# A two-layer diffusion trunk on one core: the normalisation moves from GpSimd to VectorE and ScalarE, and modulations change place

## The chip, the cores and the metric

The kernel runs on one core of one Trainium2 chip. The metric is the device time of one execution in microseconds (us). The core has five engines that run beside each other and wait for each other through semaphores: TensorE (PE in the rows, matmuls; its weight loads are PEld), VectorE (DVE), ScalarE (ACT), GpSimd (POOL) and SyncE (SP, which here only issues DMA).

## The reference

One inference step of a trunk with two layers over 128 context tokens and 128 latent tokens, `D_MODEL` 2048, all in fp32. What matters here:

```python
def _modulation(cond, w_mod, b_mod):
    m = jax.nn.silu(cond) @ w_mod + b_mod
    return [t[:, None, :] for t in jnp.split(m, N_MOD, axis=-1)]

def _layer(x, mods, lw, ctx):
    shift1, scale1, gate1, shift2, scale2, gate2 = mods
    ...
    h = _rms_norm(x, lw['norm1_g']) * (1.0 + scale1) + shift1
    gq, gk, gv, gr, glr, aq, ak, av, dqkv, dz, da, db = _split_cols(h @ lw['w_in'])
    ...
    mix = jnp.concatenate([o_gla, o_att, o_dn], axis=-1) @ lw['w_out']
    x = x + gate1 * mix
    h = _rms_norm(x, lw['norm2_g']) * (1.0 + scale2) + shift2
    ff = jnp.square(jax.nn.relu(h @ lw['w_ff1'])) @ lw['w_ff2']
    x = x + gate2 * ff
    return x, (k, v, s_gla.astype(x.dtype), s_dn.astype(x.dtype))
```

Each layer has six modulation vectors of 2048 numbers for each of two conditionings (context and latent). Each is a product of a conditioning vector with a 2048 x 2048 slice of `w_mod`.

## The kernel before

Both token sets are worked on together: a tile of activations holds 128 features by 256 tokens, and 16 such tiles ("chunks" k = 0 to 15) make up the 2048 features. A product in fp32 is made of three products in a faster format. A weight tile of 128 x 1024 is loaded (`raw`), ScalarE rounds it to `hi`, VectorE takes the residue `lo = raw - hi`; the same split of the activations gives a high part (columns 0 to 255 of `act`) and a residue (256 to 511). TensorE then does `hi` with both parts and `lo` with the high part. So each weight tile costs one instruction on ScalarE (`hi<-raw`), one on VectorE (`lo<-raw,hi`) and 24 matmuls.

In order of time: a first phase (0 to about 200 us), the mixing of layer 0 (linear attention, attention and DeltaNet chains woven with projections, to about 500), its output projection (to 592), the **first lead**, the feed-forward of layer 0 (four quarters, first product `ff1(q)`, second `ff2(q)`, to 1392), the **middle lead**, the mixing and output projection of layer 1 (to 1842), the **last lead**, and the feed-forward of layer 1.

A lead (`norm_lead`) is the start of the product behind an RMS norm. So that TensorE need not wait for the norm, the first six units (five in the middle lead) are multiplied with x times its scale alone, 12 weight tiles in all (`gl` in the rows), and brought in order afterwards. Beside this, VectorE turns the mean square (`nv`) into 1/sqrt by Newton's iteration in small steps (`n2t`, `n2y`, then `diag`, which spreads it), and `normed` makes the 16 normalised chunks that all later units need: `ht` is x times rstd, `hu` the chunk with scale and shift, and then its high part (ScalarE, `act<-hu`) and residue (VectorE, `act<-hu,act`). In `normed` GpSimd makes `ht` and half of `hu`. In the two leads ahead of a feed-forward, `sink` sends the six results through relu and square (`ffr`) at the end.

A modulation is computed in one of two ways. `mod_pe` uses TensorE with the conditioning as 32 weight columns: for each of 16 slices of `w_mod` it loads two halves (`raws`) and issues four matmuls at four column positions, a "quad", 512 columns each. The profile records two passes for each such matmul, so a quad is eight records. `mod_dv` uses VectorE: 64 multiply-and-sum instructions (`junk`, the sum goes to `part` or `modc`, each followed by a short read-out), on weights loaded as `mraw` (32 loads of 512 KB). `ONDV` names the four modulations done so: (layer, number) = (0, 5), (1, 1), (1, 0), (1, 5).

When a modulation runs is set by two queues, `modq` (TensorE) and `modv` (VectorE). `start_mod` puts one in; each weight tile of a product calls `tick()`, which adds `rate[0]` and `rate[1]` to two counters and lets a modulation do its next step when its counter reaches one. `FF0M` lists which modulations of layer 1 start in the feed-forward of layer 0, `V3`, `V4` and `V5` are values of `rate[1]`, and `DL` is the number of units of `ff1(0)` ahead of `start_mod`.

This gives the order of the program. The order on each engine is then set by the framework's scheduler when the kernel is built (`TileContext(nc, schedule_with_timeline_sim=True)`): it lets an instruction that is ready go ahead of one that is not, so that pieces of modulations come to stand between other work. A token given to matmuls (`tok`) keeps those with the same token in the order in which they were written.

Of the kernel before, what the change touches and what calls it, by code (L numbers as in the profile page):

```python
# [14 lines left out]
AF = mybir.ActivationFunctionType  # L15
ALU = mybir.AluOpType
AX = mybir.AxisListType
P = 128
# [6 lines left out]
TB = 4  # L25
NRAW = 6
GATES = (4, 5, 6, 7, 0, 1, 2, 3)
V3, V4, V5 = 0.6, 0.7, 0.4
FF0M = (1, 0, 2, 4, 3)
MX1M = (4, 3)  # L30
LATE = 3
ONDV = ((0, 5), (1, 1), (1, 0), (1, 5))
DL = (0, 2)
WIDE = (1,)
K0, K1 = 0.4, 0.7
LEAD, LEAD1, PUMP, SKIP = 6, 5, 2, 2
R1, R2, R3 = 0.9, 0.45, 0.15
# [4 lines left out]
def tile_hybrid_step(ctx: ExitStack, tc: tile.TileContext, A: dict, O: dict):  # L42
    nc = tc.nc
# [16 lines left out]
    ve, se = Timed(nc.vector, 1 / 960, 0.13), Timed(nc.scalar, 1 / 1400, 0.27)  # L60
# [20 lines left out]
    def newtok():  # L81
        ntok[0] += 1
        return f"tok{ntok[0]}"

    def mm(out, lhsT, rhs, start=True, stop=True, tok=None, **kw):
        i = nc.tensor.matmul(out, lhsT=lhsT, rhs=rhs, start=start, stop=stop, **kw)  # L86
        n = math.prod(rhs.shape[1:])
        pe_t[0] += max(n / 2400 * (1 if rhs.dtype == F32R else 4), 0.027)
        if tok is not None:
            tc.stamp_issue_order_token(i.ins, tok)  # L90
        return i
# [21 lines left out]
    def bc(ap, n):  # L113
        s = list(ap.shape)
        return ap.unsqueeze(len(s)).to_broadcast(s + [n])
# [5 lines left out]
    X = {}  # L121
# [88 lines left out]
    def load_half(src, pl=None):  # L210
        raw = (pl or wraw).tile([P, 1024], F32, tag="raw", name="raw")
        nc.sync.dma_start(raw, src)
        return raw
# [25 lines left out]
    rate = [1.0, 0]  # L239
# [94 lines left out]
    def gemm_seq(units, rhs_of, wide=False):  # L334
        for u in units:
            gemm_d([u], rhs_of, 16, wide)
# [90 lines left out]

    def mod_pe(l, m, modc, bm):
        ps = pmod.tile([P, 512], F32, tag="mod", name="mod")
        for k in range(16):  # L430
            raws = [load_half(A["w_mod"][l, m, k, half]) for half in range(2)]
            for gg in range(4):
                mm(
                    ps[32 * gg : 32 * gg + 32, :],
                    sc[:, 2 * k : 2 * k + 32],
                    raws[gg // 2][:, (gg % 2) * 512 : (gg % 2) * 512 + 512],
                    start=(k == 0),
                    stop=(k == 15),
                    tile_position=(0, 32 * gg),
                )  # L440
            yield
        msb = nrm.tile([P, 512], F32, tag="msb", name="msb")
        se.activation(msb, ps, AF.Copy)
        pt = ps
        for r in range(4):
            mm(pt[:, r * 8 : r * 8 + 8], msb[:, r * P : r * P + P], sel8)
        ve.tensor_tensor(
            modc[:, m].rearrange("p (g r) c -> p r g c", r=4),
            pt[:, 0:32].rearrange("p (r g c) -> p r g c", r=4, c=2),
            bc(bm[:, m].rearrange("p (g r) -> p r g", r=4), 2),  # L450
            ALU.add,
        )
        yield
# [38 lines left out]
    def normed(rstd, dst, scl, shf):  # L492
        for k in range(16):
            t = X["np"].tile([P, 256], F32, tag="ht", name="ht", bufs=2)
            u = X["np"].tile([P, 256], F32, tag="hu", name="hu", bufs=2)
            nc.gpsimd.tensor_tensor(t, X["x"][:, k, :], rstd, ALU.mult)  # L496
            if k % 2 == 0:
                nc.gpsimd.tensor_scalar(u[:, 0:P], t[:, 0:P], scl[:, k, 0:1], shf[:, k, 0:1], ALU.mult, ALU.add)
            else:
                se.activation(u[:, 0:P], t[:, 0:P], AF.Identity, scale=scl[:, k, 0:1], bias=shf[:, k, 0:1])  # L500
            ve.tensor_scalar(u[:, P:256], t[:, P:256], scl[:, k, 1:2], shf[:, k, 1:2], ALU.mult, ALU.add)
            se.activation(dst[:, k, 0:256], u, AF.Copy)
            ve.tensor_tensor(dst[:, k, 256:512], u, dst[:, k, 0:256].bitcast(F32), ALU.subtract)
            yield

    def norm_lead(srcs, xsp, dst, scl, shf, ldp, sink=None):
        se.activation(xsp[:, :, 256:258], shf, AF.Copy)
        ve.tensor_tensor(xsp[:, :, 514:516], shf, xsp[:, :, 256:258].bitcast(F32), ALU.subtract)
        rstd = get_rstd()
        return lead_gemm(srcs, xsp, rstd, normed(rstd, dst, scl, shf), ldp, sink)  # L510
# [5 lines left out]
    def start_mod(l, m):  # L516
        modc, s12, bm, ng = mods[l]

        def chain():
            yield from (mod_dv if (l, m) in ONDV else mod_pe)(l, m, modc, bm)  # L520
            if m in (1, 4):
                j = 0 if m == 1 else 1
                ve.scalar_tensor_tensor(
                    s12[:, j].rearrange("p k c -> p c k"), modc[:, m].rearrange("p k c -> p c k"), 1.0,
                    ng[:, j].unsqueeze(1).to_broadcast([P, 2, 16]), ALU.add, ALU.mult,
                )

        g = chain()
        gens[l, m] = g
        (modv if (l, m) in ONDV else modq).append(g)  # L530
        return g

    def tsrc(w, n):
        return lambda half: w[n, half]
# [108 lines left out]
    for l in range(L):  # L643
# [171 lines left out]
        else:  # L815
            nlead = list(zip(FIRST, first))
            for j in FIRST[len(first) : 13]:
                for _ in range(2):
                    if nlead:
                        u, ps = nlead.pop(0)  # L820
# [563 lines left out]
        x = X["x"]  # L1384
# [33 lines left out]
        last = l + 1 == L  # L1418
        hids = [act, hidb]

        def ff_evac(hid, j):
            def f(ps):
                r = X["np"].tile([P, 256], F32, tag="ht", name="ffr", bufs=2)
                r2 = X["np"].tile([P, 256], F32, tag="hu", name="ffr2", bufs=2)
                se.activation(r, ps, AF.Relu)
                se.activation(hid[:, j, 0:256], r, AF.Square)
                se.activation(r2, r, AF.Square)
                ve.tensor_tensor(hid[:, j, 256:512], r2, hid[:, j, 0:256].bitcast(F32), ALU.subtract)

            return f  # L1430

        norm_lead([tsrc(w1, j) for j in range(LEAD)], hidb, nact, s12[:, 1], modc[:, 3], X["np"],
                  lambda j, t: ff_evac(act, j)(t))
        rate[:] = [R3, V4 if last else V3]
        if not last:
            mod_tiles(l + 1)
            layer_consts(l + 1)
# [1 line left out]
        def ff1(q):  # L1439
            hid = hids[q % 2]  # L1440
            us = [(tsrc(w1, q * 16 + j), ff_evac(hid, j)) for j in range(LEAD if q == 0 else 0, 16)]
            if q == 0:
                d = DL[l]
                gemm_seq(us[:d], lambda k: nact[:, k, 0:512])
                us = us[d:]
                if (l, 5) not in gens:
                    start_mod(l, 5)
                if not last:
                    for m in FF0M:
                        start_mod(l + 1, m)  # L1450
            gemm_seq(us, lambda k: nact[:, k, 0:512])
            return hid

        def ff2(q, hid):
            st = q == 3 and not last
            sc1 = mods[l + 1][1][:, 0] if st else None
            gemm_seq([(tsrc(w2[q], n), res_evac(n, 5, act if st else None, sc1)) for n in range(16)], lambda k: hid[:, k, 0:512], l in WIDE)

        h0 = ff1(0)
        h1 = ff1(1)  # L1460
        mod_flush(gens[l, 5])
        rate[1] = 0 if last else V5
        ff2(0, h0)
        h2 = ff1(2)
        ff2(1, h1)
        h3 = ff1(3)
# [186 lines left out]
```

## Time and profile before

| what | value |
|---|---|
| time, median of 3 runs | 2616.69 us (2614.7 to 2617.31) |
| the profiled execution's own time | 2615.59 us |
| its span, first to last instruction | 2613.8 us |
| TensorE busy | 2518.4 us, 96% |
| VectorE busy | 1831.2 us, 70% |
| ScalarE busy | 1208.2 us, 46% |
| GpSimd busy | 121.4 us, 5% |
| mean granted TensorE clock | 0.986 |
| read from HBM | 612.57 MB, 237 GB/s over the span |

Matmuls are pipelined, and the ends of their records are modelled, so a stretch in which TensorE is busy throughout can still hold fewer matmuls than another. The number of records in a stretch, at the pace of a stretch where nothing waits, says how much work was done in it. The granted clock is a share of TensorE's full speed. An idle time is put down to the instruction that ended it.

### The profile page before, as it was taken

What the parts mean: (1) busy time and instruction counts of PE and PEld (TensorE: products, weight loads), DVE (VectorE), ACT (ScalarE), POOL (GpSimd) and SP (SyncE); (2) the same over time, 40 slices, a digit from 0 to 9 for tenths busy, and PEclk for the clock granted to TensorE, in tenths of its full rate; (3) what the DMA queues carried; (4) which work ended last, traced back from release to release, by engine and by line L of the source; (5) the groups of instructions that cost most, each with busy time, mean ns of one, the idle gap of its engine ahead of it and who ended that gap; (6) DMA issues with size and microseconds to landing.
All of it is one profiled execution on the core that took longest, in us unless ns stands there. A gap on an engine that the chain in (4) does not pass through costs nothing.

```text
span 2613.8 us, 47705 instructions
## 1 busy us (share of the span) xinstructions
PE 2518.4 (96%) x18860; PEld 2252.6 (86%) x18860; DVE 1831.2 (70%) x3462; ACT 1208.2 (46%) x1905; POOL 121.4 (5%) x131
## 2 busy tenths in 40 slices
PE   6999999998899999999999999999879999999999
PEld 4777677787899999999998888889869989999988
DVE  3457757799999889444567676889894565564665
ACT  3356244444554354354355653555355535445433
POOL 1000000004000000000004000000120000000000
PEclk9999999999999999999999999999979999999999
DMA  9876767897899998777776764448666666666564
GB/s 352 320 255 211 272 216 255 325 353 243 275 342 334 329 339 299 231 231 226 224 232 221 276 201 125 143 127 295 230 200 187 184 191 188 185 192 187 186 196 142
DMA packets 171937, 622.01 MB, mean 238 GB/s; under 512 B 20497, under 2 KB 21073, under 8 KB 170689
## 3 DMA queue, kind: packets, MB, share of 16 engines
q1 hardware_dynamic: 165600, 600.12, 68.3%
q0 software_dynamic: 3712, 15.59, 1.7%
q8 instruction: 148, 2.42, 0.4%
q10 hardware_dynamic: 2400, 3.24, 0.4%
q14 instruction: 77, 0.62, 0.1%
HBM read 612.57 MB, written 6.31 MB: 237 GB/s over the span
## 4 chain that ended last, share of the span: by engine, by line
PE 85%; issue 6%; DMA 5%; DVE 3%; ACT 1%; SPq 0%; ACTq 0%; DVEq 0%; POOLq 0%
PE g L86 64%; PE gt L86 6%; PE mod L86 5%; DMA raw<-w_tok 1%; DMA sb<-scd 1%; DMA raw<-w_in 1%; DMA raw<-w_mod 1%; DVE junk L56 1%; DVE lo L56 1%; PE ga L86 1%; PE gl L86 1%; PE eb L86 1%; DVE act L56 1%; ACT hi L56 0%; PE fbm L86 0%
## 5 line engine op out<-in xcount | busy, mean ns | idle before, releaser
L56 ACT ACTIVATE hi<-raw 128x1024 fp32r<-128x1024 f32 (+1 forms) x742 | 784.5, 1058 | 1097.5 <-PE g L86 799.9
L56 DVE TENSOR_TENSOR lo<-raw,hi 128x1024 fp32r<-128x1024 f32 (+1 forms) x742 | 908.8, 1225 | 444.9 <-ACT hi L56 433.5
L86 PE MATMUL g<-act,hi 128*128 128x256 f32 (+1 forms) x7488 | 1064.1, 292 | 39.6 <-DVE act L56 17.1
L86 PEld LDWEIGHTS g<-act,hi 128*128 128x128 f32 x7488 | 961.5, 190 | 119.6 <-DVE act L56 22.7
L86 PE MATMUL g<-act,lo 128*128 128x256 f32 x4000 | 563.7, 282 | 0.0
L86 PEld LDWEIGHTS g<-act,lo 128*128 128x128 f32 x4000 | 517.2, 190 | 14.8 <-issue 3.2
L56 DVE SCALAR_TENSOR_TENSOR x<-g,modc,x 128x128 f32<-128x128 f32 x448 | 142.4, 348 | 183.2 <-PE g L86 177.9
L86 PE MATMUL g<-hid,hi 128*128 128x256 f32 (+1 forms) x1536 | 261.2, 319 | 0.0
L86 PEld LDWEIGHTS g<-hid,hi 128*128 128x128 f32 x1536 | 217.0, 188 | 23.9 <-ACT hi L56 5.0
L86 PE MATMUL mod<-raw,sc 128*32 128x512 f32 (+1 forms) x1280 | 164.0, 529 | 24.8 <-DMA raw<-w_mod 20.3
L56 DVE CUSTOM_DVE_ANT_0 junk<-mraw,sb,part 128x1024 bf16<-128x1024 f32 x128 | 170.7, 1334 | 9.6 <-DMA sb<-scd 9.4
L56 DVE CUSTOM_DVE_ANT_0 junk<-mraw,sb,bm 128x1024 bf16<-128x1024 f32 x128 | 163.9, 1281 | 4.0 <-DMA sb<-scd 3.1
L86 PE MATMUL gt<-hi,act 128*128 128x512 f32 x512 | 141.4, 408 | 3.4 <-ACT hi L56 3.4
L86 PE MATMUL g<-hid,lo 128*128 128x256 f32 x1024 | 141.8, 281 | 0.0
L86 PEld LDWEIGHTS g<-hid,lo 128*128 128x128 f32 x1024 | 134.6, 188 | 5.4
L86 PEld LDWEIGHTS gt<-hi,act 128*128 128x128 f32 x512 | 94.0, 190 | 39.6 <-issue 11.7
L86 PEld LDWEIGHTS mod<-raw,sc 128*32 128x32 f32 x1280 | 31.9, 109 | 66.8 <-issue 16.8
L496 POOL TENSOR_TENSOR ht<-x,rstd 128x256 f32<-128x256 f32 x48 | 56.2, 1187 | 480.9 <-ACT rstd L56 461.8
L86 PE MATMUL gl<-hid,hi 128*128 128x258 f32 x384 | 73.9, 294 | 3.4 <-ACT hi L56 2.4
L86 PE MATMUL gt<-lo,act 128*128 128x512 f32 x256 | 75.6, 403 | 0.0
L86 PE MATMUL gl<-hid,lo 128*128 128x258 f32 x192 | 56.7, 295 | 9.4 <-DVE lo L56 9.4
L86 PEld LDWEIGHTS gl<-hid,hi 128*128 128x128 f32 x384 | 62.1, 198 | 4.1 <-ACT hi L56 2.8
(355 smaller groups left out, 1926.6 us busy)
## 6 DMA issues: line engine op xcount, KB each, us to landing
raw<-w_ff SPq DMA_DIRECT2D x512, 512.0 KB, 4.4
raw<-w_mod SPq DMA_DIRECT2D x256, 512.0 KB, 5.8
mraw<-w_modT SPq DMA_DIRECT2D x128, 512.0 KB, 5.1
raw<-w_in SPq DMA_DIRECT2D x86, 512.0 KB, 4.4
raw<-w_tok SPq DMA_DIRECT2D x64, 512.0 KB, 4.8
raw<-w_out SPq DMA_DIRECT2D x64, 512.0 KB, 4.9
sb<-scd POOLq DMA_DIRECT2D x8, 1024.0 KB, 8.9
raw<-w_in SPq DMA_DIRECT2D x16, 448.0 KB, 6.2
```

The lines of the kernel that those rows point to most:

```text
L56: return f(out, *a, **kw)
L86: i = nc.tensor.matmul(out, lhsT=lhsT, rhs=rhs, start=start, stop=stop, **kw)
L496: nc.gpsimd.tensor_tensor(t, X["x"][:, k, :], rstd, ALU.mult)
```

## The change

`normed` no longer uses GpSimd: VectorE makes `ht` as x times scale times rstd, in one instruction for each half of the tokens, and ScalarE adds the shift. The modulation (1, 5), the fourth on VectorE, starts in the feed-forward of layer 0 (`FF0M`) and no longer in that of layer 1, with `V5` raised from 0.4 to 0.55 and `V4` gone. `DL` is 2 in both layers. In `mod_pe` the quad's two matmuls on the second half of the weights come first, and all matmuls of a modulation carry one token.

```diff
-V3, V4, V5 = 0.6, 0.7, 0.4
-FF0M = (1, 0, 2, 4, 3)
+V3, V5 = 0.6, 0.55
+FF0M = (1, 0, 5, 2, 4, 3)
...
-DL = (0, 2)
+DL = 2
...
     def mod_pe(l, m, modc, bm):
         ps = pmod.tile([P, 512], F32, tag="mod", name="mod")
+        tk = newtok()
         for k in range(16):
             raws = [load_half(A["w_mod"][l, m, k, half]) for half in range(2)]
-            for gg in range(4):
+            for gg in (2, 3, 0, 1):
                 mm(
...
                     tile_position=(0, 32 * gg),
+                    tok=tk,
                 )
...
-            nc.gpsimd.tensor_tensor(t, X["x"][:, k, :], rstd, ALU.mult)
-            if k % 2 == 0:
-                nc.gpsimd.tensor_scalar(u[:, 0:P], t[:, 0:P], scl[:, k, 0:1], shf[:, k, 0:1], ALU.mult, ALU.add)
-            else:
-                se.activation(u[:, 0:P], t[:, 0:P], AF.Identity, scale=scl[:, k, 0:1], bias=shf[:, k, 0:1])
-            ve.tensor_scalar(u[:, P:256], t[:, P:256], scl[:, k, 1:2], shf[:, k, 1:2], ALU.mult, ALU.add)
+            for g in range(2):
+                s = slice(g * P, g * P + P)
+                ve.scalar_tensor_tensor(t[:, s], X["x"][:, k, s], scl[:, k, g : g + 1], rstd[:, s], ALU.mult, ALU.mult)
+                se.activation(u[:, s], t[:, s], AF.Identity, bias=shf[:, k, g : g + 1])
             se.activation(dst[:, k, 0:256], u, AF.Copy)
             ve.tensor_tensor(dst[:, k, 256:512], u, dst[:, k, 0:256].bitcast(F32), ALU.subtract)
...
-        rate[:] = [R3, V4 if last else V3]
+        rate[:] = [R3, 0 if last else V3]
...
-                d = DL[l]
+                d = DL
```

The change moves instructions on each engine. The first place is TensorE in the mixing of layer 0, where `gt` is a projection and `mod` a modulation (x4 is one quad of four matmuls). Before:

```order
L86 MATMUL gt<-hi,act 128x512 x8
L86 MATMUL mod<-raw,sc 32x512 x2
L86 MATMUL gt<-lo,act 128x512 x4
L86 MATMUL mod<-raw,sc 32x512 x2
L86 MATMUL gt<-hi,act 128x512 x8
```

And after the change:

```order
L86 MATMUL gt<-hi,act 128x512 x8
L86 MATMUL gt<-lo,act 128x512 x4
L86 MATMUL mod<-raw,sc 32x512 x4
L86 MATMUL gt<-hi,act 128x512 x8
L86 MATMUL gt<-lo,act 128x512 x4
```

The two halves of the quad, which had four matmuls of the projection between them, now stand together. Ahead of the first lead there were 61 runs of modulation matmuls (32 of them of one to three matmuls) and there are now 49 (11 of one to three), for 48 quads.

The second place is VectorE in the last lead, at the start of Newton's iteration, where `junk` is a step of the modulation (1, 5). Before:

```order
L56 TENSOR_SCALAR nv_20908<-st_20905 128x2
L56 TENSOR_TENSOR lo_21130<-raw_21127,hi_21129 128x1024
L56 ISA junk_22320,part_21674<-mraw_22245,sb_21677,bm_6790 128x1024
L56 ISA part_21674 128x1
L56 TENSOR_SCALAR n2t_20911<-nv_20908 128x2
L56 ISA junk_22322,part_21674<-mraw_22245,sb_21677,bm_6790 128x1024
```

And after the change:

```order
L56 TENSOR_SCALAR nv_21137<-st_21134 128x2
L56 TENSOR_SCALAR n2t_21140<-nv_21137 128x2
L56 TENSOR_SCALAR n2y_21139<-n2t_21140 128x2
L56 SCALAR_TENSOR_TENSOR n2t_21140<-nv_21137,n2y_21139 128x2
L56 TENSOR_TENSOR n2t_21140<-n2t_21140,n2y_21139 128x2
L56 SCALAR_TENSOR_TENSOR n2y_21139<-n2t_21140,n2y_21139 128x2
```

The steps of the modulation are gone from this lead, here and among its chunks, and Newton's steps follow each other.

The third place is the same point of the first lead, where `junk` is a step of the modulation (0, 5). Before:

```order
L56 TENSOR_SCALAR nv_6219<-st_6216 128x2
L56 TENSOR_SCALAR n2t_6222<-nv_6219 128x2
L56 TENSOR_SCALAR n2y_6221<-n2t_6222 128x2
L56 TENSOR_TENSOR lo_6441<-raw_6438,hi_6440 128x1024
L56 SCALAR_TENSOR_TENSOR n2t_6222<-nv_6219,n2y_6221 128x2
```

And after the change:

```order
L56 TENSOR_SCALAR nv_6219<-st_6216 128x2
L56 TENSOR_TENSOR lo_6401<-raw_6398,hi_6400 128x1024
L56 ISA junk_8209,modc_146<-mraw_8164,sb_8087,part_7015 128x1024
L56 ISA modc_146 128x1
L56 TENSOR_SCALAR n2t_6222<-nv_6219 128x2
L56 ISA junk_8211,modc_146<-mraw_8164,sb_8087,part_7015 128x1024
```

Here steps of the modulation have come in between Newton's steps, 12 of them up to `diag`; from there to the last chunk there are 13 where 18 stood.

## Rows read from the trace of the kernel before

**Rows 1.** The table of stretches: the leads, a full stretch, the feed-forward, the mixing.

```profile
core 0: us, PE busy (x) PEld busy (x) DVE busy (x) ACT busy (x) POOL busy (x), PEclk, DMA share, GB/s
592.50:680.00 87.50, 68.46 (x480) 60.20 (x479) 81.78 (x141) 42.99 (x93) 33.21 (x25) 0.90 0.72 235
1392.00:1447.00 55.00, 50.77 (x393) 44.85 (x392) 43.88 (x87) 34.79 (x72) 26.39 (x26) 0.99 0.70 246
1842.00:1945.00 103.00, 75.77 (x480) 70.89 (x479) 95.85 (x165) 43.19 (x93) 32.64 (x25) 0.80 0.65 209
1950.00:2050.00 100.00, 100.00 (x852) 100.00 (x851) 53.80 (x62) 55.24 (x90) 0.00 (x0) 1.00 0.62 187
700.00:1050.00 350.00, 350.00 (x2936) 333.46 (x2935) 318.20 (x457) 159.81 (x226) 1.58 (x3) 1.00 0.92 328
1050.00:1350.00 300.00, 300.00 (x2517) 286.38 (x2516) 151.87 (x209) 130.38 (x174) 0.00 (x0) 1.00 0.72 227
225.00:550.00 325.00, 322.73 (x2152) 231.59 (x2148) 235.18 (x660) 131.28 (x228) 9.28 (x16) 1.00 0.76 273
```

**Rows 2.** Waits of TensorE in the last lead: us in all, times, longest.

```profile
PE gl L86 <- DVE lo L56: 6.8, 5, 3.3
PE g L86 <- DVE act L56: 6.7, 4, 2.8
...
PE g L86 <- ACT ffr L56: 4.6, 1, 4.6
```

**Rows 3.** VectorE's groups, last lead: count | busy us, mean ns | idle us before.

```profile
L56 DVE CUSTOM_DVE_ANT_0 junk<-mraw,sb,part 128x1024 bf16<-128x1024 f32 x27 | 37.6, 1393 | 5.9 <-DMA sb<-scd 5.9
L56 DVE TENSOR_TENSOR lo<-raw,hi 128x1024 fp32r<-128x1024 f32 x20 | 26.7, 1335 | 1.0 <-ACT hi L56 0.9
L56 DVE CUSTOM_DVE_ANT_0 junk<-mraw,sb,bm 128x1024 bf16<-128x1024 f32 x13 | 16.7, 1283 | 0.0
...
L56 DVE TENSOR_SCALAR hu<-ht,s,modc 128x128 f32<-128x128 f32 x16 | 5.2, 361 | 0.0
```

**Rows 4.** Timeline of VectorE, first and last lead: start us, length us.

```profile
601.77 0.16 DVE L56 TENSOR_SCALAR nv<-st 128x2 f32<-128x2 f32 x1 [0.74 <-PE st L86]
...
605.30 0.42 DVE L56 TENSOR_TENSOR diag<-c_ident,n2y 128x256 f32<-128x256 f32 x1
...
1851.62 0.15 DVE L56 TENSOR_SCALAR nv<-st 128x2 f32<-128x2 f32 x1
...
1868.65 0.42 DVE L56 TENSOR_TENSOR diag<-c_ident,n2y 128x256 f32<-128x256 f32 x1
```

**Rows 5.** VectorE's groups, first phase (0 to 200 us).

```profile
L56 DVE SCALAR_TENSOR_TENSOR ht<-x,s,rstd 128x128 f32<-128x128 f32 x32 | 9.8, 348 | 0.5
```

**Rows 6.** ScalarE's groups in the last lead.

```profile
L56 ACT ACTIVATE ld<-ld,ldc 128x128 f32<-128x128 f32 x12 | 4.0, 390 | 0.9 <-DVE ld L56 0.9
```

**Rows 7.** VectorE's groups, 1700 to 1842 us, where GpSimd is silent.

```profile
L56 DVE TENSOR_TENSOR lo<-raw,hi 128x1024 fp32r<-128x1024 f32 x40 | 48.7, 1221 | 4.3 <-ACT hi L56 3.9 <-issue 0.3
...
L56 DVE SCALAR_TENSOR_TENSOR x<-g,modc,x 128x128 f32<-128x128 f32 x30 | 9.0, 346 | 2.3 <-PE g L86 1.8 <-DMA x<-spill 0.5
```

**Rows 8.** Waits of TensorE in the middle lead.

```profile
PE g L86 <- ACT act L56: 1.9, 1, 1.9
```

**Rows 9.** Timeline of TensorE in the mixing of layer 0, around modulation matmuls.

```profile
259.61 1.92 PE L86 MATMUL mod<-raw,sc 128*32 128x512 f32 x16
261.46 1.18 PE L86 MATMUL gt<-hi,act 128*128 128x512 f32 x4
...
276.31 1.05 PE L86 MATMUL mod<-raw,sc 128*32 128x512 f32 x2
277.29 0.66 PE L95 MATMUL tb<-c_ident,Ns 128*128 128x128 f32 x4
...
279.43 1.07 PE L86 MATMUL mod<-raw,sc 128*32 128x512 f32 x8
280.43 1.19 PE L86 MATMUL gt<-hi,act 128*128 128x512 f32 x4
```

## The prediction

> **What bounds the kernel now.** I read the page first (TensorE busy nearly throughout, its clock digit below 9 in one slice), then the table of stretches, then in the weak stretches the waits of TensorE and VectorE's groups. In [rows 1] the stretch 1950 to 2050 is the yardstick: TensorE runs 852 matmul records in 100 us at full clock, 0.1174 us each. TensorE is also busy for all of 700 to 1050 and 1050 to 1350 and for 322.7 of 325 us in 225 to 550: there its own work is the time, and whatever is taken from it there is gained. The three leads are different. At that pace their records are worth 480 x 0.1174 = 56.3 us of 87.5 (first lead), 393 x 0.1174 = 46.1 of 55 (middle) and 56.3 of 103 (last): 31.2, 8.9 and 46.7 us are lost, part of it as idle time and part because the granted clock falls to a mean of 0.90 and 0.80 in the first and last. What ends the waits is not DMA. In the last lead TensorE waits for VectorE's residues of weights and chunks and for ScalarE [rows 2], and VectorE is busy 95.9 of 103 us, 81.8 of 87.5 in the first lead, but 43.9 of 55 in the middle one, which has no modulation beside it. So the first and last leads are VectorE's, and the middle one is nearly TensorE's.
>
> **The fourth modulation leaves the last lead.** VectorE's groups there [rows 3] hold 27 + 13 modulation steps, 37.6 + 16.7 = 54.3 us, over half of its work. They also stand between the nine small steps of Newton's iteration: from the mean square to the diagonal takes 1868.65 - 1851.62 = 17.0 us, against 605.30 - 601.77 = 3.5 us in the first lead, where none stand between [rows 4]. The order after the change has no step of a modulation in this lead. New on VectorE are two scalar-tensor-tensor instructions per chunk. The first phase runs exactly this form, from the same kind of tiles, in 348 ns [rows 5]: 32 x 0.348 = 11.1 us; 16 tensor-scalars of 0.361 us (5.8) go. VectorE: 95.9 - 54.3 + 11.1 - 5.8 = 46.9 us, now under TensorE's 56.3. ScalarE gets 32 bias additions; the row of the same form has 390 ns [rows 6], 12.5 us on 43.2, at most 55.7: just under 56.3 and the tightest point. What stays lost I take from the nearest row, the middle lead, which is built alike and has no modulation steps: 8.9 us. Gain 46.7 - 8.9 = 38 us. Bounds: 46.7 (nothing stays), and 30 (the wait for a free accumulator bank, 4.6 us in [rows 2], which only the two feed-forward leads have, and as much again for ScalarE).
>
> [...]
>
> **The middle lead.** The chunks' multiplication leaves GpSimd. TensorE's 1.9 us wait for a chunk's high part [rows 8] is what I expect to go; gain 2, bounds 0 and 8.9.
>
> **The first lead keeps its modulation.** Here the change is not a relief. By the order, between the first weight residue of the lead and the last chunk and its outputs, VectorE had 26 modulation steps and now has 32, and 12 of them have moved in between Newton's steps, as in the last lead of before: the 3.5 us become about 17, so the chunks start some 13 us later. Afterwards they come faster, with 13 steps among them instead of 18. VectorE: 81.8 + 6 x 1.283 + 11.1 - 5.8 = 94.8 us; with GpSimd silent the steps shrink from 1393 to 1283 ns [rows 3] and the weight residues from 1335 to 1221 [rows 3, 7], 26 x 0.110 + 18 x 0.114 = 4.9 us. That leaves 89.9, against 87.5 us that the lead took with 5.7 us of VectorE's idle time in it. I take 3 us slower; bounds 6 faster (the chunk chain of three engines is shorter by one) and 12 slower (TensorE starves during Newton's steps and its clock falls once more).
>
> **Modulation slices unbroken.** In the first layer's mixing, a piece of two records holds TensorE as long as a whole quad of eight: 0.98 us (276.31 to 277.29) against 1.00 (279.43 to 280.43), and two quads in a row take 1.85 [rows 9]. By the order, the 48 quads ahead of the first lead stood in 61 runs, 32 of them one to three matmuls; they now stand in 49, 11 of them short. Before: 32 x 0.98 + 25 x 1.00 + 3 x 1.85 + one of twelve (2.7) = 64.6; after: 11 x 0.98 + 33 x 1.00 + 4 x 1.85 + 2.7 = 53.9. TensorE has no slack in 225 to 550, so 10.7 us are gained. Bounds: 12.7 (by the same prices, two us more in the second layer), and nothing, if a quad that now waits for both halves of its weights leaves TensorE idle instead.
>
> **The fourth modulation arrives in the first feed-forward.** 64 steps x 1.283 = 82 us of VectorE, and 32 loads of 512 KB. I cost it at nothing: in 700 to 1050 VectorE carries the first three at 318.2 of 350 us, DMA share 0.92, and TensorE loses nothing; in 1050 to 1350 VectorE has 300 - 151.9 = 148 us free, DMA share 0.72 [rows 1]. The steps are ahead of the layer's last quarter in the order, with the same density as the first three. Without that cover it costs up to 82 us. The new rates and the common start after two units only place these steps.
>
> **Sum.** -38 - 2 + 3 - 10.7 = -47.7, on the profiled execution's own 2615.6: 2567.9. The median shown is 1.1 above that execution, so 2569.
>
> **Rivals.**
> (a) *The first lead shortens too.* GpSimd is busy 33.2 us in it [rows 1]; if each of its instructions stops VectorE outright, removing it frees far more than 4.9 us, VectorE falls to about 95 - 33 = 62 us, and the lead loses only the middle lead's 8.9: 22 gained in place of 3 lost, 2544. Against it: VectorE's means differ by a tenth of a microsecond only. [...]
> (b) *ScalarE becomes the last lead's bound.* At 55.7 of 56.3 us any bubble between it and VectorE shows, and chunks have only two buffers. Half the gain goes: about 18 more, 2587. For it: TensorE already waits 4.6 us behind ScalarE's row of outputs [rows 2].
> (c) *The slices gain nothing*, each quad waiting for its later half: 2580.
> (d) *Slower: VectorE falls behind TensorE in the first feed-forward.* At 318 of 350 us it has 9% left; if the fourth modulation's steps fall where weight residues are due and not into the 148 us, each delays TensorE by its 1.283 us. All 64 exposed give 2569 + 82 = 2651; it ends slower than before once over 48 of the 82 us are exposed. Against it: three such modulations cost TensorE nothing.
>
> **Chances.** Forecast 0.66 (2555 to 2583), (a) 0.12, (b) 0.13, (c) 0.04, (d) 0.05. The range takes in (b), (c) and the bounds of the first lead, 2546 to 2592, and leaves out (d) and about half of (a). No change, within 0.2% (5.2 us, about what a measurement of this kernel can tell), has only the edge of (d) and a pile of (b), (c) and the bad bounds: 0.02. Faster 0.93, slower 0.05.
>
> **What would show it.** In the profile after: the last lead as long as the middle one relative to its records, clock near 1, VectorE clearly under TensorE, no wait over about 4 us; GpSimd nearly without busy time; in the first lead 17 us from mean square to diagonal and about 90 us in all; modulation records in runs of eight in the mixing, and some 11 us less from 225 to the first lead; VectorE near 90% busy until about 1300 with TensorE still busy throughout. I would be wrong if the last lead still lost 20 us or more, if waits for weight residues appeared between 1050 and 1350, or if the first lead moved by over 12 us either way.

## The result and the profile after

The changed kernel takes 2575.85 us (median of four runs, 2574.34 to 2589.99), the kernel before 2615.69, measured with it: ratio 0.9858, interval 0.9827 to 0.9889. In four later runs it took 2581.71 (2579.73 to 2583.36) against 2613.76: 0.9877, 0.9864 to 0.9891. So it is faster by 1.2 to 1.4%, where the forecast of 2569 was 1.8%. The first profiled execution is the slowest of these eight (2589.99); where a stage of it differs from the later profile, that is said.

Below are its span and the page's first table, and then the table of stretches with the three leads and the later part of layer 0's feed-forward. Each lead's stretch holds as many matmul records as in [rows 1], within 3.

```profile
span 2588.2 us, 47588 instructions
...
PE 2503.7 (97%) x18860; PEld 2250.6 (87%) x18860; DVE 1822.5 (70%) x3510; ACT 1225.7 (47%) x1977; POOL 31.2 (1%) x59
```

```profile
606.20:699.70 93.50, 73.09 (x483) 68.25 (x482) 84.67 (x167) 50.21 (x117) 0.53 (x1) 0.82 0.67 226
1410.40:1462.00 51.60, 50.61 (x396) 44.54 (x395) 41.22 (x98) 38.26 (x93) 1.08 (x2) 1.00 0.76 268
1858.00:1919.70 61.70, 58.04 (x483) 57.58 (x482) 47.42 (x101) 48.28 (x118) 0.00 (x0) 1.00 0.53 171
1050.00:1350.00 300.00, 300.00 (x2514) 285.42 (x2513) 225.00 (x327) 126.88 (x165) 0.53 (x1) 1.00 0.83 285
```

The last lead fell from 103 to 61.7 us for the same records, at full clock, with VectorE at 47.4 us. The middle lead fell from 55 to 51.6, and the wait for a chunk's high part [rows 8] is no longer among its waits. The first lead grew from 87.5 to 93.5, and its clock fell to 0.82. The feed-forward took the fourth modulation (VectorE 151.9 to 225.0 us in 1050 to 1350) with no loss to TensorE, 2514 records against 2517.

VectorE's groups in the last lead come first: the new instruction has the length forecast. Then come the waits of TensorE there, of which only two are left, and then the timeline of VectorE around Newton's iteration, in the first and in the last lead:

```profile
L56 DVE TENSOR_TENSOR lo<-raw,hi 128x1024 fp32r<-128x1024 f32 x20 | 24.5, 1225 | 10.6 <-ACT hi L56 10.5
L56 DVE SCALAR_TENSOR_TENSOR ht<-x,s,rstd 128x128 f32<-128x128 f32 x32 | 9.2, 348 | 0.2 <-ACT rstd L56 0.2
```

```profile
PE g L86 <- ACT ffr L56: 2.6, 1, 2.6
PE gl L86 <- ACT hi L56: 1.0, 1, 1.0
```

```profile
612.75 0.16 DVE L56 TENSOR_SCALAR nv<-st 128x2 f32<-128x2 f32 x1
613.20 1.23 DVE L56 TENSOR_TENSOR lo<-raw,hi 128x1024 fp32r<-128x1024 f32 x1 [0.28 <-ACT hi L56]
614.34 1.28 DVE L56 CUSTOM_DVE_ANT_0 junk<-mraw,sb,part 128x1024 bf16<-128x1024 f32 x1
...
615.54 0.17 DVE L56 TENSOR_SCALAR n2t<-nv 128x2 int32<-128x2 int32 x1
615.67 1.28 DVE L56 CUSTOM_DVE_ANT_0 junk<-mraw,sb,part 128x1024 bf16<-128x1024 f32 x1
...
635.64 0.42 DVE L56 TENSOR_TENSOR diag<-c_ident,n2y 128x256 f32<-128x256 f32 x1
...
1863.89 0.16 DVE L56 TENSOR_SCALAR nv<-st 128x2 f32<-128x2 f32 x1 [0.51 <-PE st L86]
...
1867.62 0.42 DVE L56 TENSOR_TENSOR diag<-c_ident,n2y 128x256 f32<-128x256 f32 x1
```

The two leads have changed roles: 22.9 us from mean square to diagonal in the first (3.5 before), 3.7 in the last (17.0 before, [rows 4]).

To set the stages of many traces side by side, this table counts from the timeline of ScalarE: every kernel rounds 742 weight tiles (`hi<-raw`), and the columns are the times between the starts of the same ones (us; the first lead is from the 121st to the 141st, the last from the 481st to the 521st, the feed-forward of layer 0 from the 141st to the 361st, the middle lead from there to the 381st). Each row is that kernel's profiled execution.

```
kernel            to 41st  mixing 0  first lead  ff 0   middle  mixing 1  last lead  rest   span
before             195.3    403.1      89.3     661.4    64.8    404.6     160.5    634.6  2613.8
after              198.5    413.6      94.1     661.4    63.3    403.7     118.9    634.6  2588.2
after_again        195.8    403.9      94.1     661.4    63.3    404.4     120.5    634.6  2577.9
slices_alone       192.0    410.5      99.0     661.4    64.2    405.5     150.5    634.6  2617.8
normed_alone       195.4    402.5      79.3     661.4    63.4    406.7     149.3    634.7  2592.8
schedule_alone     195.4    403.3      89.1     661.4    64.9    408.1     117.7    634.7  2574.6
no_slices          196.3    403.4      80.0     661.4    63.4    410.7     118.9    634.6  2568.8
hold_newton        191.2    402.1      71.1     661.4    63.3    404.0     120.5    634.6  2548.4
hold_lead          193.3    401.5      61.1     661.7    65.2    406.4     120.6    634.7  2544.5
no_slices_hold     193.9    404.2      61.1     662.8    68.5    409.2     120.4    634.7  2554.8
```

What the change was to give in the first mixing is not there: 403.9 against 403.1 us in the later execution, and 413.6 in the first one.

### The profile page after: what moved, and what is told of

Same layout as the page of the kernel before. It is cut to its first block, busy times and chain, and to the rows that moved or that the text cites. A ratio compares the mean times of both kernels' runs of the same rounds, so it can differ in the third digit from the quotient of the medians.

```text
span 2588.2 us, 47588 instructions
## 1 busy us (share of the span) xinstructions
PE 2503.7 (97%) x18860; PEld 2250.6 (87%) x18860; DVE 1822.5 (70%) x3510; ACT 1225.7 (47%) x1977; POOL 31.2 (1%) x59
## 4 chain that ended last, share of the span: by engine, by line
PE 89%; DMA 4%; DVE 3%; ACT 2%; issue 1%; SPq 0%; ACTq 0%; DVEq 0%
PE g L86 67%; PE gt L86 6%; PE mod L86 4%; PE gl L86 4%; DMA raw<-w_mod 2%; DMA raw<-w_tok 1%; DVE lo L56 1%; ACT hi L56 1%; PE ga L86 1%; DVE junk L56 1%; PE eb L86 1%; DMA raw<-w_in 1%; PE fb L86 0%; PE fbm L86 0%; PE ob L86 0%
## 5 line engine op out<-in xcount | busy, mean ns | idle before, releaser
L86 PE MATMUL mod<-raw,sc 128*32 128x512 f32 (+1 forms) x1280 | 152.1, 537 | 28.9 <-DMA raw<-w_mod 25.3
L56 DVE CUSTOM_DVE_ANT_0 junk<-mraw,sb,part 128x1024 bf16<-128x1024 f32 x128 | 164.1, 1282 | 2.1 <-DMA sb<-scd 1.7
L86 PEld LDWEIGHTS gt<-lo,act 128*128 128x128 f32 x256 | 48.3, 192 | 10.8 <-issue 0.4
```

The source lines that it names most:

```text
L56: return f(out, *a, **kw)
```

## The experiments

Each is compared with runs of the kernel before on the same chip at the same time: 2613.76 us for the first four, 2613.48 for the last four.

**after_again**: the changed kernel, unedited, for a second profile.

> The changed kernel once more, unedited. Three of its four first executions took 2574 to 2577 us, the profiled one 2590. Theory A: the profiled one met a disturbance of about 15 us ahead of the first lead, where it was 13.6 us behind the kernel before; then this execution has about 2575 us, the first lead starts near 590 to 592, and the first mixing gains 0 to 3 us and not 10.7. Theory B: the 13.6 us belong to the order of the change; then the first lead starts near 606 here too and the 15 us between executions lie elsewhere.

Measured 2581.71. The first lead starts at 593.7 us, the first mixing gains nothing: theory A for the mixing, though the time is some 7 us above the 2575 named there. Most of the 10 us by which the first execution's mixing was longer arise at two places, one stretch each in the tables of the first (upper fence) and the second execution:

```profile
236.00:276.00 40.00, 37.65 (x186) 23.17 (x185) 27.97 (x118) 17.08 (x26) 0.54 (x1) 0.91 0.59 205
476.00:516.00 40.00, 34.70 (x242) 25.78 (x241) 22.06 (x52) 16.11 (x32) 3.23 (x6) 0.91 0.86 322
```

```profile
236.00:276.00 40.00, 37.84 (x189) 23.30 (x189) 31.39 (x139) 15.86 (x20) 0.54 (x1) 1.00 0.69 240
476.00:516.00 40.00, 36.37 (x278) 27.53 (x277) 28.72 (x65) 16.43 (x32) 3.22 (x6) 1.00 1.02 395
```

In the first execution the granted clock fell to a mean of 0.91 in both, and in the later stretch 242 records were done in place of 278. TensorE waits a little in these stretches in both executions. But the falls are no accident of the first execution alone, as theory A has it. Of the five profiled executions with the new order of the slices, four (after, slices_alone, hold_newton, hold_lead) have 0.91 in the stretch 236 to 276: the granted clock is 0.50 for 6.8 us, just behind the same wait of TensorE (`qkb`, below). The first execution falls twice more and slices_alone once more near 500 us. Of the five with the old order none falls between 198 us and its first lead. So the falls come with the new order, and cost 3.4 to 6.8 us ahead of the first lead where they come; why after_again was spared is open.

**slices_alone**: of the change, only the modulation slices.

```diff
+        tk = newtok()
...
-            for gg in range(4):
+            for gg in (2, 3, 0, 1):
...
+                    tok=tk,
```

> The kernel before with only the modulation slices on TensorE in unbroken order. By the prediction's sum 10.7 us in the first mixing and 2 in the second layer: 2603 to 2606. By the reading of the result (the first mixing gains next to nothing): 2612 to 2617, and the first lead starts at 590 to 594 as before (592.5).

Measured 2623.45, ratio 1.0037 (1.0025 to 1.0050): slower, which neither reading had. In the table 7.4 us are lost in the first mixing (5.1 of them by the clock) and 9.7 in the first lead, where the mean square to the diagonal takes 21.9 us; the last lead is 10.0 us shorter, with 15 modulation steps in place of 17 between its diagonal and its last chunk. So this part, and neither of the others, puts the steps of modulation (0, 5) between Newton's in the first lead. The effect is the halves' order alone: with the token but the old order, the program is row for row that of the kernel before on every engine; with the new order and no token it is that of this run.

**normed_alone**: of the change, only `normed`.

```diff
-            nc.gpsimd.tensor_tensor(t, X["x"][:, k, :], rstd, ALU.mult)
...
+                ve.scalar_tensor_tensor(t[:, s], X["x"][:, k, s], scl[:, k, g : g + 1], rstd[:, s], ALU.mult, ALU.mult)
+                se.activation(u[:, s], t[:, s], AF.Identity, bias=shf[:, k, g : g + 1])
```

> The kernel before with only the normalisation on VectorE and ScalarE. Theory A (VectorE's work sets the lead, and the fourth modulation is still in the last one): VectorE has 95.9 + 5.3 us less about 8 for steps that no longer share with GpSimd, so the last lead stays within 4 us of 103 and the time is 2608 to 2618. Theory B (GpSimd is what holds the last lead up): the last lead falls by 20 us or more, 2596 or less.

Measured 2590.45, 0.9914 (0.9900 to 0.9927). The time lies where theory B put it, but neither theory's account holds: 10.0 us go in the first lead and 11.2 in the last, where B wanted 20 or more; each of the two still has its modulation. 1.4 go in the middle lead.

In the first lead the gain arises between the diagonal and the last chunk: 56.4 us before, 46.2 here. VectorE's groups in that time, before (605.3 to 661.7, upper three) and in this run (604.8 to 651):

```profile
L56 DVE CUSTOM_DVE_ANT_0 junk<-mraw,sb,part 128x1024 bf16<-128x1024 f32 x18 | 27.0, 1500 | 3.5 <-DMA sb<-scd 3.5
L56 DVE TENSOR_TENSOR lo<-raw,hi 128x1024 fp32r<-128x1024 f32 x11 | 15.6, 1423 | 0.0
L56 DVE TENSOR_SCALAR hu<-ht,s,modc 128x128 f32<-128x128 f32 x16 | 5.4, 354 | 0.0
...
L56 DVE CUSTOM_DVE_ANT_0 junk<-mraw,sb,part 128x1024 bf16<-128x1024 f32 x14 | 17.9, 1280 | 1.5 <-DMA sb<-scd 1.5
L56 DVE TENSOR_TENSOR lo<-raw,hi 128x1024 fp32r<-128x1024 f32 x11 | 13.4, 1219 | 0.0
L56 DVE SCALAR_TENSOR_TENSOR ht<-x,s,rstd 128x128 f32<-128x128 f32 x32 | 9.6, 347 | 0.0
```

GpSimd's groups in the same lead of the kernel before, and in the last lead of schedule_alone, where no modulation stands:

```profile
L496 POOL TENSOR_TENSOR ht<-x,rstd 128x256 f32<-128x256 f32 x16 | 16.6, 1050 | 17.1 <-DVE hu L56 8.0 <-ACT rstd L56 7.2 <-issue 1.5
L498 POOL TENSOR_SCALAR hu<-ht,s,modc 128x128 f32<-128x128 f32 x8 | 16.2, 2019 | 7.1 <-DVE act L56 5.5 <-DMA mraw<-w_modT 1.6
```

```profile
L496 POOL TENSOR_TENSOR ht<-x,rstd 128x256 f32<-128x256 f32 x16 | 18.8, 1195 | 105.0 <-ACT rstd L56 104.4
L498 POOL TENSOR_SCALAR hu<-ht,s,modc 128x128 f32<-128x128 f32 x8 | 5.4, 680 | 0.0
```

VectorE sets the pace of the chunks. Its only idle time there, 3.5 and 1.5 us, is a wait for a load of `sb`, while GpSimd is idle for 24.2 us, 13.5 of them behind VectorE's `hu` and `act`. So the gain is VectorE's: the modulation steps take 9.1 us less, because four of them now come behind the last chunk and the others shrink from 1500 to 1280 ns; the weight residues take 2.2 less, and 2.0 of idle time go; against it `ht` takes 9.6 where `hu` took 5.4.

The forecast had 1393 and 1335 ns for the stretched steps and residues. These are means of two lengths, as a piece of both timelines of the kernel before shows, VectorE first and then GpSimd:

```profile
613.44 1.79 DVE L56 CUSTOM_DVE_ANT_0 junk<-mraw,sb,part 128x1024 bf16<-128x1024 f32 x1
...
615.16 1.74 DVE L56 TENSOR_TENSOR lo<-raw,hi 128x1024 fp32r<-128x1024 f32 x1
...
617.50 1.28 DVE L56 CUSTOM_DVE_ANT_0 junk<-mraw,sb,part 128x1024 bf16<-128x1024 f32 x1
```

```profile
613.41 2.41 POOL L496 TENSOR_TENSOR ht<-x,rstd 128x256 f32<-128x256 f32 x2 [1.49 <-DVE hu L56]
617.42 1.52 POOL L498 TENSOR_SCALAR hu<-ht,s,modc 128x128 f32<-128x128 f32 x1 [1.59 <-DMA mraw<-w_modT]
```

Where the two engines overlap, one or the other is long. Beside the two `ht` it is VectorE's step and residue, by half a microsecond; the step at 617.50 keeps its length, and GpSimd's `hu` takes 1.52 us. Of the 29 steps in the lead eight take 1.74 to 1.79 us and 20 take 1.27 to 1.29. GpSimd's `hu` (a quarter of all `hu`, not half) takes 2019 ns here, 1508 in the last lead and 680 without a modulation beside it; its `ht` does not grow (1050, 1270 and 1195).

**schedule_alone**: of the change, only the fourth modulation in the first feed-forward.

```diff
-FF0M = (1, 0, 2, 4, 3)
+FF0M = (1, 0, 5, 2, 4, 3)
...
-        rate[:] = [R3, V4 if last else V3]
+        rate[:] = [R3, 0 if last else V3]
```

(with `V5` and `DL` as in the change.)

> The kernel before with only the fourth modulation in the first feed-forward (with its rates and the common start after two units). Theory A (VectorE's 54.3 us of modulation steps were the last lead's loss): the last lead falls by 30 to 40 us even with GpSimd in it, VectorE there near 42 us, 2576 to 2588, and the feed-forward of layer 0 keeps its 710 us. Theory B (GpSimd's chunks set the lead as soon as the steps are gone): the lead stays 15 us or more above TensorE's 56, 2593 or more.

Measured 2575.36, 0.9851 (0.9836 to 0.9866): theory A, a little below its range. The last lead falls by 42.8 us with GpSimd still in it; the feed-forward keeps its 661.4. Only layer 1's mixing grows, by 3.5. The whole change took 2581.71 on the same chip at the same time, 6 us more than this part alone: the other two parts together gained nothing.

**no_slices**: the whole change without the part of slices_alone.

> The changed kernel with the modulation slices on TensorE as before. If the three parts add up: the schedule's 42.9 us in the last lead, the normalisation's 10.5 in the first lead and about 2 in the middle one, 2555 to 2563, 15 to 25 us faster than the whole change; from mean square to diagonal 3.5 us in the first lead. Rival: the fourth modulation together with the normalisation makes the 23 us between Newton's steps, and the slices have no part in it; then 2570 to 2582.

Measured 2570.58, 0.9832 (0.9817 to 0.9847). Mean square to diagonal is 3.5 us and the first lead 80.0, so the rival's cause is out, though the time lies in the rival's range: it is 8 us over the upper end of theory A, 6 of them in layer 1's mixing (410.7 against 404.6), which I had not counted. Against after_again the slices' order costs 14.1 us in the first lead and gives 6.3 back in layer 1's mixing.

**hold_newton** and **hold_lead**: the whole change, and modulation (0, 5) can't begin before the first lead's rstd is there, or before its last chunk. Its bias is written once more, with zero times that value added, so the steps wait for the write.

```diff
+        if hold is not None:
+            ve.scalar_tensor_tensor(hold, rstd[:, 0:16], 0.0, hold, ALU.mult, ALU.add)
```

```diff
+        if l == 0:
+            bm5 = mods[0][2][:, 5, :]
+            ve.scalar_tensor_tensor(bm5, nact[:, 15, 0:16].bitcast(F32), 0.0, bm5, ALU.mult, ALU.add)
```

> The whole change, with the steps of modulation (0, 5) held back until rstd of the first lead is there. Theory A (the steps between Newton's are what the first lead pays for): mean square to diagonal 3.5 us again, the first lead 8 to 15 us shorter than with the whole change, 2563 to 2574. Theory B (VectorE's amount of work sets the lead, wherever its steps stand): within 3 us of the whole change, 2575 to 2583.

> The whole change, with the steps of modulation (0, 5) held back until the last chunk of the first lead. Theory A (VectorE's work is the first lead's loss as it was the last lead's, and the feed-forward has room): VectorE near 50 us in the lead, the lead 25 us shorter than with the whole change, the feed-forward of layer 0 unchanged at 710 us with some 40 us more of VectorE in it, 2550 to 2560. Rival: the modulation comes late for the second quarter's flush or crowds the residues there, the feed-forward gets longer by 10 us or more, 2562 or more.

hold_newton: 2554.36, 0.9772 (0.9759 to 0.9785), theory A's cause, and 9 us below its range: mean square to diagonal 3.7 us, the lead 23.0 us shorter than with the whole change. The hold also moves the 34 steps that ran ahead of Newton's, but from diagonal to last chunk 12 steps stand where 13 stood, and the last chunk comes 53.5 us after the lead's start where it came after 72.1: the 18.6 us between are, within a microsecond, what the diagonal comes sooner after the mean square (19.2). hold_lead: 2549.68, 0.9759 (0.9742 to 0.9777), theory A at the lower end of its range; the lead loses another 10.0 us with those 12 steps. Its table of stretches, first lead and feed-forward:

```profile
588.50:651.00 62.50, 59.79 (x496) 58.42 (x495) 56.06 (x117) 49.08 (x118) 0.00 (x0) 1.00 0.65 206
651.00:1000.00 349.00, 349.00 (x2927) 333.42 (x2926) 315.75 (x451) 163.04 (x235) 2.12 (x4) 1.00 0.92 328
1000.00:1300.00 300.00, 300.00 (x2514) 285.42 (x2514) 272.96 (x409) 126.60 (x165) 1.59 (x3) 1.00 0.92 331
```

The first lead is now as the last one of the change: full clock, 496 records in 62.5 us. All four modulations run in the feed-forward, VectorE 273.0 of 300 us busy in its second stretch, and TensorE still loses nothing. By its median this is the fastest kernel of the study, though its interval overlaps that of hold_newton. Over the runs the first lead goes with its last chunk: this one comes 68.8 us after the lead's start before, 72.1 in the change, 58.5 in normed_alone, 77.9 in slices_alone and 42.0 here, and the lead in the table is 19 to 22 us longer each time.

**no_slices_hold**: hold_lead with the slices as before.

> The hold to the last chunk with the slices as before. Theory A (the two effects add up): 10 to 20 us below the version without the slices' part, 2538 to 2550. Rival: once Newton's steps are free, VectorE's work in the first lead costs nothing more, 2553 to 2563.

Measured 2557.19, 0.9787 (0.9774 to 0.9801): its own profile shows theory A's lead (61.1 us against 80.0 in no_slices), but the total is 7 us above the range that I gave, and in the rival's. Against no_slices it gains 13 us, which is within the 10 to 20 of theory A; its middle lead grows by 5.1 us, for a reason that is open. Beside hold_lead it is the cleanest comparison of the slices, since neither has a modulation step in the first lead: here the new order is 7.5 us faster (the two intervals overlap by a little).

The waits of TensorE from 200 to 592 us show the other side of the new order: after_again first, then no_slices_hold, whose two rows are all that it has:

```profile
PE g L86 <- ACT hi L56: 3.4, 4, 1.4
PE g L86 <- DVE lo L56: 3.2, 3, 1.6
PE g L86 <- DVE x L56: 2.1, 1, 2.1
PE qkb L86 <- ACT E L56: 1.8, 1, 1.8
PE mod L86 <- DMA raw<-w_mod: 1.2, 2, 1.0
PE oatb L86 <- ACT pT L56: 1.1, 1, 1.1
```

```profile
PE g L86 <- DVE act L56: 0.4, 1, 0.4
PE g L86 <- ACT act L56: 0.2, 1, 0.2
```

In the timeline of TensorE from 198 to 592 us the pieces of slices can be counted, each up to the next matmul or to TensorE's idle time. They hold it 64.8 us in 61 pieces before, 54.0 in 49 in after_again, 66.6 in 63 in no_slices_hold and 55.0 in 49 in hold_lead. Its idle time there goes the other way: 2.3, 13.1, 0.6 and 8.5 us.

The wait of `qkb` for `E` can be followed on ScalarE, in the kernel before (upper fence) and in after_again, with TensorE's row last:

```profile
233.08 0.58 ACT L56 ACTIVATE E<-db 128x512 f32<-128x512 f32 x1
233.55 0.62 ACT L56 ACTIVATE t<-t 128x512 f32<-128x512 f32 x1
234.36 0.60 ACT L56 ACTIVATE E<-db 128x512 f32<-128x512 f32 x1 [0.19 <-PE db L86]
234.97 1.28 ACT L56 ACT_TABLE_LOAD   x1
```

```profile
235.14 0.57 ACT L56 ACTIVATE E<-db 128x512 f32<-128x512 f32 x1
235.62 0.61 ACT L56 ACTIVATE t<-t 128x512 f32<-128x512 f32 x1
236.25 1.28 ACT L56 ACT_TABLE_LOAD   x1
237.55 0.63 ACT L56 ACTIVATE t<-t 128x512 f32<-128x512 f32 x1
238.20 1.28 ACT L56 ACT_TABLE_LOAD   x1
239.49 0.60 ACT L56 ACTIVATE E<-db 128x512 f32<-128x512 f32 x1
...
240.14 1.16 PE L86 MATMUL qkb<-dqk 128*128 128x128 f32 x8 [1.77 <-ACT E L56]
```

With the old order both `E` come ahead of the table load; with the new one the scheduler has put a `t` and two table loads between them, and they begin 4.35 us apart in place of 1.28. All five profiled executions with the new order have this and a wait of 1.6 to 2.4 us; the five with the old order have 1.0 to 1.3 us and no wait. No piece of a modulation stands at this place in either. The waits for `pT` and `x` are alike: before, the matmuls `ga` and `obg` stood between `ptb` and `oatb`, and VectorE took `x` ahead of the weight residues; in after_again neither is so.

The waits for `hi` and `lo` are in the output projection. There the DMA engines are full, with a share of 1.01 (before) and 1.02 (after_again) from 516 to 556 us, and ScalarE's `hi` waits for weights, up to 5.3 and 4.3 us; 275 and 265 matmul records are done. With modulation (0, 5) held back, its loads are not there yet, and the new order does gain: 310 records in hold_lead (share 0.93) against 272 in no_slices_hold (0.88). The hold also takes the steps from VectorE, so this does not tell loads and steps apart.

## Why the prediction was right, and where it was not

- **The last lead: right.** Forecast 38 us, measured 41.6 and 40.0. schedule_alone has all of it, so the cause is the 40 steps. The other two parts, each alone, shorten this lead too (10.0 and 11.2 us) while the steps are in it, and add nothing once they are gone. VectorE's 47.4 us are close to the 46.9 forecast. The new instruction's 348 ns are those of [rows 5]. ScalarE's new bias additions did not become the bound: only 2.6 us of wait behind its outputs, against 4.6 in [rows 2]; rival (b) is out.
- **The middle lead: right.** 2 forecast, 1.5 measured.
- **The fourth modulation's cover: right.** 661.4 us of feed-forward before and after; even with modulation (0, 5) moved in as well it is 661.7. Rival (d) is out. The sign that VectorE would be near 90% busy until 1300 did not come (225.0 of 300 us).
- **The first lead: the sum came out by luck.** 3 us slower forecast, 4.8 measured. Two terms were too small and nearly cancel. The steps between Newton's cost 19.4 us from mean square to diagonal, where some 13 were forecast. From diagonal to last chunk 56.4 us became 43.0, a gain of 13.4, where the forecast had 4.9 for the relief from GpSimd and 13 steps among the chunks for 18; normed_alone by itself gains 10.2 there. In the sum the lead's length was VectorE's work, 89.9 us, but VectorE was busy for 84.7 of 93.5: what counted was when the chunks were done. By parts, the lead gains 10.0 (normed_alone; 9.3 in no_slices) and loses 14.1 (no_slices to after_again; 9.7 in slices_alone, with GpSimd still there). Rival (a), that the lead shortens, was right in its direction for GpSimd's part and half right in its size (22). Its condition, that each of GpSimd's instructions stops VectorE outright, no run shows: the step at 617.50 kept its 1.28 us beside GpSimd's `hu`. But the means, a tenth of a microsecond apart, hid single instructions lengthened on either side (1.79 us for 1.28 on VectorE, 1.52 for 0.68 on GpSimd). What lengthens them was not tried.
- **The slices: the step that failed.** "TensorE has no slack in 225 to 550, so 10.7 us are gained." The price held: the pieces hold TensorE 10.8 us less. The conclusion did not: 10.8 us of idle time appear in the same stretch, and nothing is gained in the first mixing. About 5 of them are waits behind ScalarE and VectorE, whose programs the scheduler ordered otherwise around the unbroken quads (`qkb`, `oatb`, `x`); the forecast had looked at TensorE's order alone. Some 7 are in the projection, where the weight loads were all but the pace already (DMA share 1.01 before, 516 to 556 us). There, as I read it, the short pieces had lain in the time of these waits; that was not tried by itself. The falls of the clock (3.4 to 6.8 us where they come) are on top. Rival (c) had the right number for this term, for a wrong reason: the quads' own wait for their weights is 1.2 us of it. Part of the waits in the projection goes with modulation (0, 5): held back, it leaves no wait for a residue there, and the idle time falls from 13.1 to 8.5.

after_again's profiled execution gains 35.9 us of the 47.7 forecast, and the slices' 10.7 is most of what is missing. The total lies in the forecast's range because that was wide enough for rival (c). Left open: why layer 1's mixing is up to 6 us longer in kernels with the schedule and the old slices, and the 6 us between the two medians of the changed kernel.

## What to carry to other kernels

Where a scheduler orders the program, an edit on one engine can reorder the others: here a new order of matmuls saved TensorE 10.8 us and brought as much idle time, part of it from two table loads that came between two exponentials on ScalarE. So compare the order on every engine, not only on the one that was edited. In this kernel work on the engine that paces a stage cost most where a short serial chain stood in its queue: twelve steps inside a chain of small instructions cost 14 us (no_slices to after_again) to 23 (hold_newton to after_again, where other steps move too), the same number beside the chunks 10. When a co-working engine is to be removed, look at the lengths of single instructions in the stretch that sets the time: a mean over the stage hid that some of them took 1.4 times as long.

## What the hardware showed that was not expected

A GpSimd tensor-scalar of 128x128 took 680 ns in a lead without modulation on VectorE, and 1508 and 2019 ns beside it; VectorE's 128x1024 steps beside GpSimd came in two lengths, 1.27 to 1.29 and 1.74 to 1.79 us, which a mean of 1393 ns does not show. Two table loads of 1.28 us between two exponentials on ScalarE were enough for a wait of TensorE of 1.6 to 2.4 us, and in four of five executions its granted clock was 0.50 for 6.8 us just behind it.
